# Stick-breaking scores: the second products on 64 rows, in both row halves of the TensorE array

## The chip, the cores and the metric

The kernel runs on one core of a Trainium2 chip. The metric is the device time of one execution in microseconds, lower is better. The profiler records one execution, with the start and duration of each instruction on each engine: TensorE (PE for matmuls, PEld for its weight loads), VectorE (DVE), ScalarE (ACT), GpSimd (POOL) and SyncE (SP, which issues DMAs).

## The reference

One decoder layer on a sequence of 512 tokens with 1024 channels. Two attention branches, eight heads of 64 channels each, work on the same modulated input; the change touches the second one, stick-breaking attention:

```python
z = jnp.einsum('bhqd,bhkd->bhqk', qi, k).astype(jnp.float32) * ATTN_SCALE
strict = kpos[None, :] < qpos[:, None]
log_beta = jax.nn.log_sigmoid(z)
log_one_minus = jnp.where(strict, jax.nn.log_sigmoid(-z), 0.0)
rest = lax.cumsum(log_one_minus, axis=3, reverse=True) - log_one_minus
a = jnp.where(strict, jnp.exp(log_beta + rest), 0.0)
return jnp.einsum('bhqk,bhkd->bhqd', a.astype(v.dtype), v)
```

The other branch (FoX) is softmax attention whose logits get a decay `c_t - c_s` per head. Both branches are projected, gated, merged and projected again; then come a LayerNorm, a gated MLP with a causal convolution of width 3, and a second LayerNorm. All in 32-bit floats.

## The kernel before

Every matmul operand is split in two numbers of the matmul format (fp32r): a high part, written by ScalarE (`hi_of`), and a low part, the difference to the original, written by VectorE (`lo_of`). A product is then the sum of high times high, low times high and high times low; low times low is left out. A projection (`mm3`, line 140) is three matmuls for each of eight pieces of 128 rows, each with 128 x 128 weights and 512 moving columns.

For attention scores a head has only 64 channels, so the 128 rows of the array hold two parts at once. For a stick-breaking head (`br` is 1):

- `s1`, 128 rows, from q: rows 0 to 63 the high part, rows 64 to 127 the low part (`q_half`; `s2` is the same tile).
- `m1`, 128 rows, from k: the high part twice (`k_half`).
- `m2`, 68 rows: the low part of k in rows 0 to 63, and zeros in rows 64 to 67.

The first product, `s1` by `m1` over 128 rows, gives (high q + low q) times high k. The second one, over 68 rows, adds high q times low k. The four rows beyond 64 hold the decay in the FoX branch, which shares this code; in the stick-breaking branch they are filled with zeros (`m2z` for heads 0 and 1, `m2t` for the others, which FoX heads use later).

Queries come in four blocks `i` of 128, of which causality needs 128, 256, 384 and 512 keys; the products are never narrower than 256 columns, so their widths are 256, 256, 384 and 512. They lie in three PSUM banks: bank 2 holds blocks 1 and 0, bank 0 holds block 2, bank 1 holds block 3 (`OFS`, `ROWS`). `scores` makes one bank: for each of its blocks the first product, then the second (lines 522 and 523). `sigmoids` then takes two sigmoids of a bank on ScalarE, and `scan` makes the running product and the weights on VectorE.

Heads run in order: stick-breaking 0 to 7, then FoX 0 to 7. Heads 0 and 1 are scored in a hand-written sequence before the main loop, where a helper (line 70, `Pinned`) records each engine's instructions and keeps them in program order; so their instructions appear under line 70. In the main loop each turn scores the head two ahead (`stage_a`), transposes the weights of the next head (`stage_b`, `turn`, line 585) and multiplies the present head's weights by v (`stage_c`, line 613). Between these, `fill(n)` issues n matmuls from a stream of other work: the projections of later heads, gates, branch projections. The projections' results are split as soon as they are whole (`q_evac`, `k_evac`); six matmuls later (`LEAD`) the pair's first head is scored.

Of the kernel before, what the change touches and what calls it, by code (L numbers as in the profile page):

```python
# [9 lines left out]
F32R = mybir.dt.float32r  # L10
BF16 = mybir.dt.bfloat16
AF = mybir.ActivationFunctionType
ALU = mybir.AluOpType
# [3 lines left out]
P = 128  # L17
# [31 lines left out]
def layer_kernel(ctx: ExitStack, tc: tile.TileContext, out, xT, x, crow, wa0, wa1, w1, wct, wv, bf,  # L49
# [25 lines left out]
    V, S, PE, G = Pinned(nc.vector), Pinned(nc.scalar), Pinned(nc.tensor), Pinned(nc.gpsimd)  # L75
# [10 lines left out]
    def nm(s):  # L86
        cnt[0] += 1
        return f"{s}_{cnt[0]}"

    def bank():  # L90
        return pp.tile([P, 512], F32, name=nm("ps"), tag="ps")
# [4 lines left out]
    def fl(ap):  # L96
        return ap.bitcast(F32)

    def hi_of(o, i, scale=1.0):
        S.activation(o, i, AF.Copy, scale=scale)  # L100

    def lo_of(o, i, hi):
        return V.tensor_tensor(o, i, fl(hi), ALU.subtract)  # L103
# [28 lines left out]
    def z(dt, s, shape=(P, 512)):  # L132
        return zp.tile(list(shape), dt, name=nm(s), tag="z", bufs=NZ)
# [23 lines left out]
    def weights(i, ahead=AHEAD):  # L157
        load()
        while state["proc"] < min(len(items), i + 1 + ahead):
            process()  # L160
            load()
        return items[i][4]
# [194 lines left out]
    OFS = ((2, 256), (2, 0), (0, 0), (1, 0))  # L357
    WID = (384, 512, 384)
    ORD = (1, 0, 2, 3)
    m2z = [z(F32R, "m2z", (68, 512)) for _ in range(2)]  # L360
    for t in m2z:
        G.memset(fl(t[64:68, :]), 0.0)
    ptc, s2t, m2t, chi, atp = [], [], [], [], []

    def open_att():
        att = st2.enter_context(tc.tile_pool(name="att", bufs=1, reuse_waits="tile"))
        atp.append(att)
        ptc.extend([att.tile([P, 512], F32R, name=f"ptc{i}{e}", tag=f"ptc{i}{e}") for e in range(2)] for i in range(2))
        s2t.extend(att.tile([68, 512], F32R, name=f"s2_{i}", tag=f"s2_{i}") for i in range(4))
        m2t.extend(att.tile([68, 512], F32R, name=f"m2_{i}", tag=f"m2_{i}") for i in range(4))  # L370
        chi.append(att.tile([NH, 2, 512], F32R, name="chi", tag="chi"))

    def fill_att():
        for t in ptc[0]:
            G.memset(fl(t[:, 0:128]), 0.0)
        for t in m2t[2:] + m2t[:2]:
            G.memset(fl(t[64:68, :]), 0.0)
        for t in ptc[1]:
            G.memset(fl(t[:, 0:128]), 0.0)
        for t in s2t:  # L380
            G.memset(fl(t[64:68, :]), 1.0)
            G.memset(fl(t[64:66, :]), -1.0)
# [31 lines left out]
    hd = {}  # L414
# [3 lines left out]
    def slot_free(n):  # L418
        assert n < 4 or n - 4 in scored
        return n % 4  # L420

    def idx(br, h):
        return h if br == 1 else NH + h

    def q_half(br, p, ps, hh):
        h = 2 * p + hh
        r = slice(64 * hh, 64 * hh + 64)
        s1 = z(F32R, "s1")
        hi_of(s1[0:64, :], ps[r, :], 0.125)
        d = hd.setdefault((br, h), {})  # L430
        d["s1"] = s1
        if br == 0:
            s2 = s2t[slot_free(idx(br, h))]
            G.dma_start(s2[0:64, :], s1[0:64, :])
            d["s2"] = s2
        else:
            d["s2"] = s1

        def low():
            V.scalar_tensor_tensor(s1[64:128, :], ps[r, :], 0.125, fl(s1[0:64, :]), ALU.mult, ALU.subtract)  # L440
        return low

    def k_half(br, p, ps, hh):
        h = 2 * p + hh
        r = slice(64 * hh, 64 * hh + 64)
        m1 = z(F32R, "m1")
        hi_of(m1[0:64, :], ps[r, :])
        hi_of(m1[64:128, :], ps[r, :])
        n = slot_free(idx(br, h))
        m2 = m2z[h] if br == 1 and h < 2 else m2t[n]  # L450
        lo_of(m2[0:64, :], ps[r, :], m1[0:64, :])
        d = hd.setdefault((br, h), {})
        d["m1"], d["m2"] = m1, m2

# [57 lines left out]

    ROWS = ((2,), (3,), (1, 0))

    def scores(br, h, b):
        d = hd[(br, h)]
        bk = d.setdefault("bk", {})[b] = bank()
        for i in ROWS[b]:
            o = OFS[i][1]
            w = max(256, (i + 1) * P)  # L520
            tb = slice(i * P, (i + 1) * P)
            PE.matmul(bk[:, o : o + w], d["s1"][:, tb], d["m1"][:, 0:w], start=i > 0, stop=False)  # L522
            PE.matmul(bk[:, o : o + w], d["s2"][0:68, tb], d["m2"][0:68, 0:w], start=False, stop=i != 1)  # L523

    def sigmoids(h, b):
        d = hd[(1, h)]
        bk = d["bk"].pop(b)
        om, pt = z(F32, "om"), z(F32, "pt")
        w = WID[b]
        S.activation(om[:, 0:w], bk[:, 0:w], AF.Sigmoid, scale=-1.0)  # L530
        d["last"] = S.activation(pt[:, 0:w], bk[:, 0:w], AF.Sigmoid)
        d.setdefault("om", {})[b] = om
        d.setdefault("pt", {})[b] = pt

    def scan(h, b):
        d = hd[(1, h)]
        om, pt, w = d["om"].pop(b), d["pt"][b], WID[b]
        if b == 2:
            G.memset(om[:, 256:257], 0.0)
        d0 = om[:, 1:w][:, ::-1]  # L540
        d1 = idz[:, 513 - w : 512] if b < 2 else idd[:, 1:w]
        V.tensor_tensor_scan(d0, d0, d1[:, ::-1], 0.0, ALU.mult, ALU.add)
        V.tensor_tensor(pt[:, 0 : w - 1], pt[:, 0 : w - 1], om[:, 1:w], ALU.mult)
        G.memset(pt[:, w - 1 : w], 0.0)

    def mark_scored(br, h):
        scored.add(idx(br, h))
        if br == 0 and h + 4 < NH:
            decay_rows(h + 4)
        if br == 1 and h >= 4 and gated:  # L550
            decay_rows(h - 4)

    def stage_a(br, h):
        for b in (2, 0, 1):
            scores(br, h, b)
        if br == 0:
            d = hd[(br, h)]
            bk = d.pop("bk")
            pt = d["pt"] = [z(F32, "pt"), z(F32, "pt"), z(F32, "pt")]
            sm = atp[0].tile([P, 12], F32, name=nm("sm"), tag="sm", bufs=3)  # L560
            for i in ORD:
                b, o = OFS[i]
                w = (i + 1) * P
                c = slice(o, o + w)
                V.tensor_tensor_reduce(pt[b][:, c], bk[b][:, c], negt[:, 512 - w : 512], -1.0, -NEG, ALU.add, ALU.min, sm[:, i : i + 1])
                S.activation(pt[b][:, c], pt[b][:, c], AF.Exp, bias=sm[:, i : i + 1], scale=-1.0, accum_out=sm[:, 4 + i : 5 + i])
            V.reciprocal(sm[:, 8:12], sm[:, 4:8])
            for i in ORD:
                b, o = OFS[i]
                c = slice(o, o + (i + 1) * P)  # L570
                V.tensor_scalar_mul(pt[b][:, c], pt[b][:, c], sm[:, 8 + i : 9 + i])
        else:
            for b in (2, 0, 1):
                sigmoids(h, b)
                scan(h, b)
        mark_scored(br, h)
# [271 lines left out]
    for hh in range(2):  # L848
        q_half(1, 0, grp[0], hh)()
        k_half(1, 0, grp[1], hh)  # L850
    first_mm(KT - 1, (2,))
    scores(1, 0, 2)
    first_mm(KT - 1, (7,))
    st0.close()
    open_att()
    sigmoids(0, 2)
    v_copy(0)
    scan(0, 2)
    scores(1, 0, 0)
    sigmoids(0, 0)  # L860
    scan(0, 0)
# [39 lines left out]
    for n, (b, h) in enumerate(heads):  # L901
        f1, f2, f3 = FILL[n // 8]
        if n + 2 < 16:
            if n % 2 == 0:
                fill_to(marks[(n // 2 + 1, "k")])
                fill(LEAD)
                f1 -= LEAD
            if n == 6:
                forget(hd[heads[n + 1]]["last"])
            stage_a(*heads[n + 2])  # L910
        fill(f1)
        if n + 1 < 16:
            stage_b(*heads[n + 1])
        if n == 3:
            for j in range(NB):
                v_evac(1, j, 1, vf[j])
        fill(f2)
        stage_c(b, h)
        if n == 7:
            lim[0] = marks["y0"]  # L920
        if n == 15:
            lim[0] = len(stream)
        fill(f3)
# [120 lines left out]
    for n in range(2 * FT):  # L1044
        if n < NSPLIT:
            h, l = items[wui[n]][4]
            ps = bks[n]
            up_mm(ps, h, l, slice(256, 512))
        else:
            ps = bank()  # L1050
            h, l = weights(wui[n])
# [3 lines left out]
        t = z(F32, "cv")  # L1055
# [4 lines left out]
        if n % 2 == 1:  # L1060
# [4 lines left out]
            a, b = z(F32R, "hh"), z(F32R, "hl")  # L1065
# [9 lines left out]
    for i in range(2):  # L1075
        t = fin.tile([P, D], F32, name=f"ln2_{i}", tag=f"ln2_{i}")
# [12 lines left out]
    for j in range(FT - LATE):  # L1089
        w = weights(wdi[j])  # L1090
# [4 lines left out]
    for i in range(NB):  # L1095
        tb = slice(i * P, (i + 1) * P)
        r = x1[i]
# [5 lines left out]
        for n, (e, c0, c1) in enumerate(pieces):  # L1103
            sole = (i, e) == own
            ps = bank()[:, 0 : c1 - c0] if sole else acc[i][e]
            for q in range(LATE):
                w = [ws[q][a][e][:, c0:c1] for a in range(2)]
# [8 lines left out]
        for e, c0, c1 in pieces:  # L1116
            c = slice(e * 512 + c0, e * 512 + c1)
            v = r[e][:, c0:c1]
            V.scalar_tensor_tensor(v, v, mu, lnr[0][:, c], ALU.subtract, ALU.mult)
        for e, c0, c1 in pieces:  # L1120
            c = slice(e * 512 + c0, e * 512 + c1)
# [71 lines left out]
```

## Time and profile before

| | |
|---|---|
| median of 3 runs | 753.81 us (753.63 to 754.15) |
| profiled execution, its time | 753.64 us |
| profiled execution, its span | 751.5 us |
| TensorE matmul busy | 741.8 us (99%), 3502 matmuls |
| weight loads busy | 621.0 us (83%) |
| VectorE busy | 545.4 us (73%) |
| ScalarE busy | 351.9 us (47%) |
| GpSimd busy | 126.6 us (17%) |

The span runs from the first to the last instruction of the program. Busy time is the time in which at least one instruction of the engine is on record; matmuls are pipelined, so the records of successive ones overlap, and the time that one costs is the distance to the start of the next. In a row of the timeline stand the start, the duration, the engine, the line, the operation, and what is written from what, by the program's names without their numbers (`m` stands for `m1` and `m2`, `s` for `s1` and `s2`).

### The profile page before, as it was taken

To read this page: it belongs to the slowest core of one execution; us is meant where nothing else is said; L and a number is where in the kernel's file an instruction comes from. 1 tells how busy PE (TensorE), PEld (TensorE's weight loads), DVE (VectorE), ACT (ScalarE), POOL (GpSimd) and SP (SyncE) were. 2 spreads that over 40 slices of the span, in tenths; PEclk is the share of its full clock that TensorE was granted. 3 is DMA by queue.
4 is the path that set the end of the run, shared out by engine and by line. 5 is a ranking of instruction groups with operands and counts; after the bars stand their busy time and mean duration, and the time that the engine had idled before them with its cause. 6 is when DMAs were issued, how large, how long until landed. Compare 5 with 4: busy or idle time off the path is not lost.

```text
span 751.5 us, 9515 instructions
## 1 busy us (share of the span) xinstructions
PE 741.8 (99%) x3502; PEld 621.0 (83%) x3502; DVE 545.4 (73%) x896; ACT 351.9 (47%) x587; POOL 126.6 (17%) x153
## 2 busy tenths in 40 slices
PE   9999999999999999999999999999999999999995
PEld 7888888888888888888898888888888888888885
DVE  7888989867688875596987787666755686334666
ACT  5578767468655754343246344444444442212300
POOL 2103000030110000000000690000000137454400
PEclk9999999999999999999999999999999999999998
DMA  9941332424333434565234524333333234224102
GB/s 352 405 142 70 99 139 87 157 84 168 106 114 120 154 113 168 169 232 165 86 113 140 168 94 131 139 114 133 120 117 107 85 110 149 104 86 140 56 33 79
DMA packets 31088, 100.46 MB, mean 134 GB/s; under 512 B 4113, under 2 KB 4641, under 8 KB 31042
## 3 DMA queue, kind: packets, MB, share of 16 engines
q1 hardware_dynamic: 29536, 97.69, 37.3%
q0 software_dynamic: 1504, 2.17, 1.2%
q8 instruction: 27, 0.44, 0.2%
q14 instruction: 19, 0.16, 0.1%
q10 hardware_dynamic: 2, 0.00, 0.0%
HBM read 96.63 MB, written 2.11 MB: 131 GB/s over the span
## 4 chain that ended last, share of the span: by engine, by line
PE 97%; DVE 2%; DMA 0%; ACT 0%; issue 0%; DVEq 0%
PE ps L140 56%; PE ps L330 5%; PE ps L1086 5%; PE ps L1084 5%; PE ps L1085 5%; PE ps L613 3%; PE ps L70 2%; PE ps L585 2%; PE ps L795 2%; PE ps L796 2%; PE ps L794 2%; PE ps L523 1%; PE ps L522 1%; PE ps L496 1%; PE ps L497 1%; PE ps L498 1%
## 5 line engine op out<-in xcount | busy, mean ns | idle before, releaser
L103 DVE TENSOR_TENSOR wl<-raw,wh 128x1024 fp32r<-128x1024 f32 (+1 forms) x99 | 133.2, 1346 | 55.4 <-ACT wh L100 55.2
L140 PE MATMUL ps<-u2h,wh 128*128 128x512 f32 (+1 forms) x376 | 141.2, 376 | 0.0
L140 PE MATMUL ps<-u2l,wh 128*128 128x512 f32 (+1 forms) x376 | 141.0, 376 | 0.0
L140 PE MATMUL ps<-u2h,wl 128*128 128x512 f32 (+1 forms) x376 | 133.6, 376 | 0.0
L100 ACT ACTIVATE wh<-raw 128x1024 fp32r<-128x1024 f32 (+1 forms) x99 | 103.5, 1048 | 62.7 <-PE ps L1086 46.1
L140 PE MATMUL ps<-uh,wh 128*128 128x512 f32 x213 | 84.1, 395 | 0.0
L140 PE MATMUL ps<-ul,wh 128*128 128x512 f32 x213 | 83.3, 391 | 0.0
L140 PEld LDWEIGHTS ps<-u2h,wh 128*128 128x128 f32 x376 | 70.8, 188 | 12.9
L140 PEld LDWEIGHTS ps<-u2l,wh 128*128 128x128 f32 x376 | 70.8, 188 | 12.6
L140 PEld LDWEIGHTS ps<-u2h,wl 128*128 128x128 f32 x376 | 70.4, 188 | 12.9
L140 PE MATMUL ps<-uh,wl 128*128 128x512 f32 x213 | 78.9, 390 | 0.0
L683 POOL TENSOR_TENSOR raw<-raw,gt 128x1024 f32<-128x1024 f32 x22 | 56.4, 2571 | 92.6 <-DMA raw<-in_wdn 85.0
L1057 DVE SCALAR_TENSOR_TENSOR cv<-ps,cw,cv 128x511 f32<-128x511 f32 x44 | 32.9, 748 | 53.4 <-ACT cv L1056 53.4
L1056 ACT ACTIVATE cv<-ps,cw 128x512 f32<-128x512 f32 x44 | 34.1, 776 | 45.7 <-PE ps L140 45.7
L1084 PE MATMUL ps<-wh,hh 128*128 128x512 f32 x128 | 49.8, 389 | 0.0
L1085 PE MATMUL ps<-wl,hh 128*128 128x512 f32 x128 | 49.8, 389 | 0.0
L1086 PE MATMUL ps<-wh,hl 128*128 128x512 f32 x128 | 49.8, 389 | 0.0
L140 PEld LDWEIGHTS ps<-uh,wl 128*128 128x128 f32 x213 | 40.0, 188 | 8.7
L140 PEld LDWEIGHTS ps<-uh,wh 128*128 128x128 f32 x213 | 40.0, 188 | 8.0
L140 PEld LDWEIGHTS ps<-ul,wh 128*128 128x128 f32 x213 | 40.1, 188 | 7.9
L100 ACT ACTIVATE hh<-cv 128x512 fp32r<-128x512 f32 x22 | 13.9, 633 | 57.5 <-DVE cv L1064 57.5
L216 DVE SCALAR_TENSOR_TENSOR ada<-ada,cbc 128x1024 f32<-128x1024 f32 x24 | 29.3, 1219 | 9.1 <-DMA ada<-in_wa 8.7
(245 smaller groups left out, 1428.7 us busy)
## 6 DMA issues: line engine op xcount, KB each, us to landing
raw<-in_wup SPq DMA_DIRECT2D x44, 512.0 KB, 3.4
raw<-in_wct SPq DMA_DIRECT2D x29, 512.0 KB, 3.8
ada<-in_wa SPq DMA_DIRECT2D x24, 512.0 KB, 4.3
raw<-in_wdn SPq DMA_DIRECT2D x22, 512.0 KB, 3.3
wa<-in_wa SPq DMA_DIRECT2D x16, 512.0 KB, 7.4
raw<-in_wp SPq DMA_DIRECT2D x8, 512.0 KB, 3.3
raw<-in_wo SPq DMA_DIRECT2D x8, 512.0 KB, 4.0
raw<-in_wa SPq DMA_DIRECT2D x8, 512.0 KB, 3.3
```

The source lines that it names most:

```text
L100: S.activation(o, i, AF.Copy, scale=scale)
L103: return V.tensor_tensor(o, i, fl(hi), ALU.subtract)
L140: PE.matmul(ps, w, u, start=first and n == 0, stop=last and n == 2)
L216: V.scalar_tensor_tensor(wt, wt, 1.0, cbc, ALU.mult, ALU.mult, accum_out=raw)
L330: PE.matmul(grp[g], w, u, start=j == 0 and n == 0, stop=j == KT - 1 and n == (1 if g == 7 else 2))
L613: PE.matmul(ps[:, to : to + w], v_part(br, h, j), src[e][:, so : so + w], start=a == 0 and j == 0, stop=a == 1 and j == 3)
L683: G.tensor_tensor(r, r, gt[1], ALU.mult)
L1056: S.activation(t, ps, AF.Identity, bias=cw[:, n, 3:4], scale=cw[:, n, 2:3])
L1057: V.scalar_tensor_tensor(t[:, 1:], ps[:, 0:511], cw[:, n, 1:2], t[:, 1:], ALU.mult, ALU.add)
L1084: PE.matmul(ps, hh[j][:, tb], w[0], start=first, stop=False)
L1085: PE.matmul(ps, hh[j][:, tb], w[1], start=False, stop=False)
L1086: PE.matmul(ps, hl[j][:, tb], w[0], start=False, stop=last)
```

## The change

In all stick-breaking heads the second product has 64 rows in place of 68, and the zero fills of rows 64 to 67 go. In heads 2 to 7 (`split`) the parts are also laid out so that the second products of the four blocks stand in alternating halves of the array: `s1` has, for its first 256 columns (blocks 0 and 1), the low part in rows 0 to 63 and the high part in rows 64 to 127, and for blocks 2 and 3 as before; `m2t` has 128 rows, with the low part of k a second time, for 256 columns, in rows 64 to 127. So the second products of blocks 2 and 3 use rows 0 to 63, those of blocks 1 and 0 rows 64 to 127. `scores2` issues all products of a head in an order of its own: block 1 first, 0 first, 2 first, 2 second (upper half), 1 second (lower half), 3 first, 3 second (upper), 0 second (lower). The sigmoids of heads 2 to 7 go by banks 0, 2, 1 in place of 2, 0, 1.

```diff
-    m2z = [z(F32R, "m2z", (68, 512)) for _ in range(2)]
-    for t in m2z:
-        G.memset(fl(t[64:68, :]), 0.0)
+    m2z = [z(F32R, "m2z", (64, 512)) for _ in range(2)]
...
-        m2t.extend(att.tile([68, 512], F32R, name=f"m2_{i}", tag=f"m2_{i}") for i in range(4))
+        m2t.extend(att.tile([P, 512], F32R, name=f"m2_{i}", tag=f"m2_{i}") for i in range(4))
...
-        for t in m2t[2:] + m2t[:2]:
-            G.memset(fl(t[64:68, :]), 0.0)
...
+    def split(br, h):
+        return br == 1 and h > 1
...
-        hi_of(s1[0:64, :], ps[r, :], 0.125)
         d = hd.setdefault((br, h), {})
         d["s1"] = s1
+        cut = 256 if split(br, h) else 0
+        parts = [(o, slice(a, b)) for o, a, b in ((64, 0, cut), (0, cut, 512)) if a < b]
+        for o, c in parts:
+            hi_of(s1[o : o + 64, c], ps[r, c], 0.125)
...
-            V.scalar_tensor_tensor(s1[64:128, :], ps[r, :], 0.125, fl(s1[0:64, :]), ALU.mult, ALU.subtract)
+            for o, c in parts:
+                V.scalar_tensor_tensor(s1[64 - o : 128 - o, c], ps[r, c], 0.125, fl(s1[o : o + 64, c]), ALU.mult, ALU.subtract)
...
         lo_of(m2[0:64, :], ps[r, :], m1[0:64, :])
+        if split(br, h):
+            lo_of(m2[64:128, 0:256], ps[r, 0:256], m1[64:128, 0:256])
...
+        n = 64 if br == 1 else 68
         for i in ROWS[b]:
...
+            PE.matmul(o, d["s1"][:, tb], d["m1"][:, 0:w], start=i > 0, stop=False)
+            PE.matmul(o, d["s2"][0:n, tb], d["m2"][0:n, 0:w], start=False, stop=i != 1)
+
+    def scores2(h):
+        d = hd[(1, h)]
+        bk = d["bk"] = {b: bank() for b in (2, 0, 1)}
+        for i, r in ((1, -1), (0, -1), (2, -1), (2, 0), (1, 64), (3, -1), (3, 0), (0, 64)):
+            o, tb, w = block(bk, i)
+            if r < 0:
+                PE.matmul(o, d["s1"][:, tb], d["m1"][:, 0:w], start=i > 0, stop=False)
+            else:
+                PE.matmul(o, d["s1"][r : r + 64, tb], d["m2"][r : r + 64, 0:w], start=False, stop=i != 1)
...
     def stage_a(br, h):
-        for b in (2, 0, 1):
-            scores(br, h, b)
+        if split(br, h):
+            scores2(h)
+        else:
+            for b in (2, 0, 1):
+                scores(br, h, b)
...
-            for b in (2, 0, 1):
+            for b in (0, 2, 1) if h > 1 else (2, 0, 1):
                 sigmoids(h, b)
                 scan(h, b)
```

More of the change, by code (lines that the diff above doesn't have):

```diff
@@ L513, in layer_kernel, with block @@
     ROWS = ((2,), (3,), (1, 0))
+    def block(bk, i):
+        b, o = OFS[i]
+        w = max(256, (i + 1) * P)
+        return bk[b][:, o : o + w], slice(i * P, (i + 1) * P), w
     def scores(br, h, b):
         d = hd[(br, h)]
-        bk = d.setdefault("bk", {})[b] = bank()
+        bk = d.setdefault("bk", {})
+        bk[b] = bank()
+        n = 64 if br == 1 else 68
         for i in ROWS[b]:
[L519 to L523, printed above, removed]
+            o, tb, w = block(bk, i)
[5 more added lines that the diff above has]
+        for i, r in ((1, -1), (0, -1), (2, -1), (2, 0), (1, 64), (3, -1), (3, 0), (0, 64)):
+            o, tb, w = block(bk, i)
+            if r < 0:
+                PE.matmul(o, d["s1"][:, tb], d["m1"][:, 0:w], start=i > 0, stop=False)
+            else:
+                PE.matmul(o, d["s1"][r : r + 64, tb], d["m2"][r : r + 64, 0:w], start=False, stop=i != 1)
     def sigmoids(h, b):
```

## The prediction

> **What bounds the kernel now.** I read the page first (engines, slices, chain), then the stages where stick-breaking scores are made, then TensorE's instructions in order of time.
>
> ```profile
> span 751.5 us, 9515 instructions
> PE 741.8 (99%) x3502; PEld 621.0 (83%) x3502; DVE 545.4 (73%) x896; ACT 351.9 (47%) x587; POOL 126.6 (17%) x153
> PE   9999999999999999999999999999999999999995
> PEclk9999999999999999999999999999999999999998
> PE 97%; DVE 2%; DMA 0%; ACT 0%; issue 0%; DVEq 0%
> 0.00:94.00 94.00, 92.28 (x420) 75.82 (x421) 80.43 (x151) 63.21 (x115) 17.45 (x64) 1.00 0.57 214
> 94.00:180.00 86.00, 86.00 (x428) 72.83 (x427) 69.61 (x118) 54.59 (x105) 10.09 (x32) 1.00 0.37 125
> ```
>
> The fifth line is the chain that ended last: 97% of it is TensorE. The last two lines are stages; after each stage's length stand the busy times of PE, PEld, DVE, ACT and POOL. From 94 to 180 us TensorE is never idle, at the full clock. So the end is set by how closely matmuls follow each other. A busy time can't show that, because the records overlap, so I read starts. This is the score block of head 5 in the timeline (start us, duration us, engine, line, operation, out<-in, rows and columns of the weights, shape of the moving operand, count):
>
> ```profile
> 109.58 0.39 PE L140 MATMUL ps<-ul,wh 128*128 128x512 f32 x1
> 109.81 0.28 PE L522 MATMUL ps<-m,s 128*128 128x256 f32 x1
> 109.92 0.29 PE L523 MATMUL ps<-m,s 68*128 68x256 f32 x1
> 110.04 0.29 PE L522 MATMUL ps<-m,s 128*128 128x256 f32 x1
> 110.17 0.28 PE L523 MATMUL ps<-m,s 68*128 68x256 f32 x1
> 110.28 0.34 PE L522 MATMUL ps<-m,s 128*128 128x384 f32 x1
> 110.46 0.34 PE L523 MATMUL ps<-m,s 68*128 68x384 f32 x1
> 110.64 0.40 PE L522 MATMUL ps<-m,s 128*128 128x512 f32 x1
> 110.87 0.40 PE L523 MATMUL ps<-m,s 68*128 68x512 f32 x1
> 111.11 0.40 PE L140 MATMUL ps<-uh,wh 128*128 128x512 f32 x1
> ```
>
> From start to start, 256 columns take (110.28 - 109.81) / 4 = 0.12 us, 384 take 0.18 and 512 take 0.23 to 0.24. The block takes 111.11 - 109.81 = 1.30 us. A 68-row product takes as long as a 128-row one: the unused rows save nothing. The duration of a record (0.39 for 512 columns) is 0.16 us longer than its pitch; that tail lies under the next matmul.
>
> **What the change removes.** In heads 2 to 7 the second products (L523) have 64 rows, and two of the four stand in the lower half of the array: block 1 (256 columns) behind block 2 (384), and block 0 (256) behind block 3 (512). If the halves work at once, the two 256-column products cost nothing: 2 x 0.12 = 0.24 us a head. For less: the weight loads of the second of each pair may come late.
>
> ```profile
> 109.58 0.19 PEld L522 LDWEIGHTS ps<-m,s 128*128 128x128 f32 x1
> 109.81 0.19 PEld L523 LDWEIGHTS ps<-m,s 68*128 68x128 f32 x1
> 109.92 0.19 PEld L522 LDWEIGHTS ps<-m,s 128*128 128x128 f32 x1
> ```
>
> Each load starts when the matmul ahead of it starts (109.81, 109.92), and they follow at 0.11 us. If this holds for halves too, the second of a pair starts 0.11 us after the first: the first pair then takes 0.11 + 0.11 = 0.22 in place of 0.18 + 0.12, saving 0.08; the second takes the longer of 0.22 and 0.24, saving 0.12. That is 0.20 a head. Six heads: 1.2 us, at most 1.44, and nothing if the halves don't work at once. I take 1.2, the sum by the rows of loads. The Trainium skill, page "TensorE: Matmul & The Clock Gate", Part 3, says that a load for other row groups overlaps running matmuls and that packed matmuls start some 4 ns apart; by that the saving would be about 1.4. No run here shows it.
>
> **What the change adds on TensorE.** The array passes from 128-row work to 64-row work and back. In heads 2 to 7 there are two stretches of 64 rows to a block, so 4 passages, 24 in all. Less visible: heads 0 and 1 also get 64-row second products (n is 64 wherever br is 1), and there each stands alone between 128-row products: 8 products, 16 passages, without any pairing to pay for them. So 40. No matmul of 64 rows is in this trace, so a passage has no row. The nearest rows are those where the stream breaks and a weight load can't be made ahead:
>
> ```profile
> 51.00 0.33 PE L70 MATMUL ps<-m2z,s 68*128 68x384 f32 x1
> 51.47 0.50 PE L70 MATMUL ps<-m,s 128*128 128x512 f32 x1
> 51.81 0.40 PE L70 MATMUL ps<-m2z,s 68*128 68x512 f32 x1
> 51.47 0.19 PEld L70 LDWEIGHTS ps<-m,s 128*128 128x128 f32 x1 [0.46 <-ACT pt L70]
> 59.13 1.25 PE L70 MATMUL ps<-idz,pt 128*128 128x128 f32 x10
> 60.14 0.48 PE L70 MATMUL ps<-uh,wh 128*128 128x512 f32 x1
> 60.45 0.40 PE L70 MATMUL ps<-ul,wh 128*128 128x512 f32 x1
> ```
>
> The load at 51.47 waited for ScalarE. Its matmul then took 51.81 - 51.47 = 0.34 to the next start, against 0.23: a load that isn't hidden costs 0.11. Behind the ten transposes (59.13) it is 60.45 - 60.14 = 0.31, so 0.08. Bounds of a passage: nothing, if the next load and matmul run on as now (a gain is excluded, since a passage takes no column away); and 0.16 + 0.11 = 0.27, if the next load waits until the last record has ended (0.39 - 0.23 = 0.16) and then is itself exposed. I take 0.11, the nearest row and near the middle. Two passages, around head 0's 384-column product at 51.00, lie ahead of the 0.46 us for which loads wait anyway; 38 are on the path: 38 x 0.11 = 4.2 us.
>
> **What it adds and moves elsewhere.** The rows are from the same timeline (in brackets the idle time before and what ended it), the last one from the groups by line. Per split head: one more ScalarE instruction (the high part of q in two halves of 256), and two more on VectorE (the low part of q in two, and low k once more for 256 columns).
>
> ```profile
> 62.34 1.18 ACT L70 ACTIVATE s<-ps 64x512 fp32r<-64x512 f32 x2
> 66.03 1.41 DVE L70 SCALAR_TENSOR_TENSOR s<-ps,s 64x512 fp32r<-64x512 f32 x2
> 67.46 0.68 DVE L70 TENSOR_TENSOR m<-ps,m 64x512 fp32r<-64x512 f32 x1
> 68.18 1.20 ACT L70 ACTIVATE m<-ps 64x512 fp32r<-64x512 f32 x2 [3.44 <-DVE m L70]
> 69.90 1.32 ACT L70 ACTIVATE vv<-vf 128x256 fp32r<-128x256 f32 x4
> 70.34 1.43 DVE L70 TENSOR_TENSOR vv<-vf,vv 128x256 fp32r<-128x256 f32 x4 [0.23 <-ACT vv L70]
> 70.37 0.29 PE L523 MATMUL ps<-m,s 68*128 68x256 f32 x1
> 102.52 1.13 DVE L543 TENSOR_TENSOR pt<-pt,om 128x383 f32<-128x383 f32 x2
> 114.58 1.25 PE L585 MATMUL ps<-idz,pt 128*128 128x128 f32 x10
> L523 PEld LDWEIGHTS ps<-m,s 68*128 68x128 f32 x56 | 10.5, 190 | 0.9 <-DVE m L103 0.5
> ```
>
> At 256 columns ScalarE takes 1.32 / 4 = 0.33 and VectorE 1.43 / 4 = 0.36. Head 2 is the tightest: its low k ends at 67.46 + 0.68 = 68.14 and is first used at 70.37, so 2.2 us stand between. The new VectorE work ahead of it is 4 x 0.36 - 1.41 = 0.03 for both heads' q and 0.36 for k, so 0.4; even if a 256-column instruction cost as much as one of 512 columns (0.70), it would be 4 x 0.70 - 1.41 + 0.68 = 2.1. ScalarE's two further instructions (4 x 0.33 - 1.18 = 0.14) fall before its wait of 3.44. Over six heads VectorE gets some 2.2 us in stretches where it is 81% (69.61 of 86) busy, and loads of L523 waited for it only 0.5 us in all 56. I cost this at nothing; without its cover it would be at most those 2.2 us.
>
> The order of products and of sigmoids changes: block 2's bank is now whole first, at 0.12 + 0.12 + 0.18 + 0.18 = 0.6 us after the block's start in place of 0.48 for the first bank, and the others at the end. Attention weights of head 4 (scored at 97 us) are ready at 102.52 + 1.13 = 103.65 and transposed at 114.58: 10.9 us of cover for some tenths. The six zero fills of four rows that go were on POOL, busy 17%; nothing waits for them on the path, so nothing is gained. No DMA is added, and neither SP's nor POOL's queue is passed by one.
>
> **Sum.** -1.2 + 4.2 = +3.0 us. The profiled execution took 753.64 us, 2.1 more than its span of 751.5; it becomes 756.6. The median of the runs shown, 753.81, lies 0.17 above it: 756.8.
>
> **Rivals.**
> *A, the passages cost nothing (not slower).* For it: 68-row products follow 128-row ones without any break (109.92, 110.17), and TensorE's loads already run under other matmuls. Against it: those 68-row records keep the pitch of the whole array, so they don't show a passage. It decides from 1.2 / 38 = 0.03 us a passage down; at nothing the time is 753.8 - 1.2 = 752.6, at best 752.4.
> *B, each passage waits for the array to run empty.* A matmul then starts where the one ahead ends: 38 x 0.16 = 6.1, less 1.2, so +4.9 and 758.7; with the load exposed too, 38 x 0.27 = 10.3, so +9.1 and 762.9. For it: nothing in the rows; against it: no other change of shape in the trace (transposes to matmuls) costs as much. The Trainium skill, page "TensorEngine Tiling (Array Packing)", section "Tiling Modes", says that a change of the mode, not of the tile, drains the engine; by that rule B would be the outcome. No run here shows it.
> *C, the change doesn't do what it says:* the halves run one after the other. Then +4.2 and 758.0, or 753.8 if passages are free.
> *D, VectorE's added work becomes the bound:* score loads wait for low k, up to the 2.2 us that VectorE gets over six heads; with free passages 753.8 - 1.2 + 2.2 = 754.8. Against it: the slack of 2.2 us at the tightest head, where only 0.4 is added.
>
> **How the numbers follow.** Two tenths of a per cent, 1.5 us, is what a measurement of this kernel can tell from no change. Chances: forecast 0.37, own range 754.5 to 757.9 (passages of 0.05 to 0.14); A 0.35; B 0.15; C 0.09; D 0.04. Slower from (1.5 + 1.2) / 38 = 0.07 us a passage: 0.33 of the forecast, all of B, 0.06 of C and 0.01 of D, 0.55. Within: 0.04 of the forecast, 0.21 of A, and the rest of C and D, 0.31. Faster by more than 1.5 needs A with nearly all of 1.44 and a little besides: 0.14. The range goes from A's best, 752.3, to beyond B's smaller price, 759.8; B's larger price and a few tails, under 0.2, are left out.
>
> **What will show it.** In a block of heads 2 to 7: the two 64-row records of a pair start within 0.05 us of each other if the halves work at once and the loads come early, 0.11 apart if each waits for its load, 0.18 and 0.23 if the halves take turns. The block now lasts 1.30 us; 1.10 without passages' cost, 1.54 by forecast (4 x 0.11), 1.7 to 2.2 by B. In heads 0 and 1, the start after each 64-row product: 0.12, 0.18 or 0.23 if free. VectorE's waits by score loads should stay near 0.5 us. A passage price under 0.07 us, or a saving larger than 0.24 us a head, makes the forecast wrong.

## The result and the profile after

The changed kernel takes 758.88 us (median of 6 runs, 758.61 to 759.09) against 754.01 for the kernel before beside it: a ratio of 1.0063, 95% interval 1.0051 to 1.0076. It is slower by 4.9 us. The page, its first lines and its chain:

```profile
span 757.2 us, 9533 instructions
PE 747.8 (99%) x3502; PEld 620.4 (82%) x3502; DVE 550.3 (73%) x908; ACT 354.4 (47%) x593; POOL 124.5 (16%) x147
PE 98%; DVE 1%; issue 0%; DVEq 0%; ACT 0%
```

The number of matmuls is the same, the span is 5.7 us longer and TensorE's busy time 6.0. TensorE is still the chain. So its own stream became longer; busy time even counts the loss as work. The score block of head 5, in the timeline (matmuls first, then weight loads; `x2`, `x3` are records that overlap, merged):

```profile
113.72 0.39 PE L140 MATMUL ps<-ul,wh 128*128 128x512 f32 x1
113.95 0.57 PE L541 MATMUL ps<-m,s 128*128 128x256 f32 x3
114.45 0.44 PE L543 MATMUL ps<-m,s 64*128 64x384 f32 x2
114.82 0.49 PE L541 MATMUL ps<-m,s 128*128 128x512 f32 x1
115.24 0.50 PE L543 MATMUL ps<-m,s 64*128 64x512 f32 x2
115.67 0.50 PE L140 MATMUL ps<-uh,wh 128*128 128x512 f32 x1
116.01 0.40 PE L140 MATMUL ps<-ul,wh 128*128 128x512 f32 x1
113.72 0.53 PEld L541 LDWEIGHTS ps<-m,s 128*128 128x128 f32 x3
114.44 0.19 PEld L543 LDWEIGHTS ps<-m,s 64*128 64x128 f32 x2 [0.19 <-issue]
114.81 0.19 PEld L541 LDWEIGHTS ps<-m,s 128*128 128x128 f32 x1 [0.18 <-issue]
115.24 0.19 PEld L543 LDWEIGHTS ps<-m,s 64*128 64x128 f32 x2 [0.24 <-issue]
115.67 0.19 PEld L140 LDWEIGHTS ps<-uh,wh 128*128 128x128 f32 x1 [0.24 <-issue]
115.78 0.19 PEld L140 LDWEIGHTS ps<-ul,wh 128*128 128x128 f32 x1
```

Both things happen. The pairs run at once: two loads of 0.19 us stand within 0.19 us, and two matmuls, of 384 and 256 columns, within the 0.44 of the longer. And at each passage (114.44, 114.81, 115.24, 115.67) the load no longer starts with the matmul ahead, to run under it: it starts together with the matmul that needs it, behind a gap that no wait explains ("issue"). The block, 1.30 us before, takes 115.67 - 113.95 = 1.72, and the projection behind it starts with an exposed load (one that no matmul hides): 116.01 - 115.67 = 0.34 in place of 0.24, 0.10 more. That is 0.52 a head.

In heads 0 and 1, where nothing runs at once, the passages stand alone:

```profile
50.12 0.28 PE L70 MATMUL ps<-m,s 128*128 128x256 f32 x1
50.32 0.38 PE L70 MATMUL ps<-m2z,s 64*128 64x256 f32 x1
50.63 0.38 PE L70 MATMUL ps<-m,s 128*128 128x256 f32 x1
50.95 0.38 PE L70 MATMUL ps<-m2z,s 64*128 64x256 f32 x1
51.26 0.50 PE L70 MATMUL ps<-uh,fpad 128*128 128x512 f32 x1
51.59 0.40 PE L70 MATMUL ps<-ul,fpad 128*128 128x512 f32 x1
```

256 columns, 0.12 us before, now take 0.31 to 0.32 from start to start, in both directions (the first, whose own load is still hidden, 0.20). The first products of heads 0 and 2 in the kernel before, then head 2's in the changed one:

```profile
49.87 0.28 PE L70 MATMUL ps<-m,s 128*128 128x256 f32 x1
70.26 0.28 PE L522 MATMUL ps<-m,s 128*128 128x256 f32 x1
72.92 0.57 PE L541 MATMUL ps<-m,s 128*128 128x256 f32 x3
```

From head 0's first product to head 2's first, 70.26 - 49.87 = 20.39 us before, it is now 72.92 - 50.12 = 22.80: 2.4 us lost. With 6 x 0.52 = 3.1 that makes 5.5, and the 0.25 by which head 0 starts later in this execution makes the 5.7 of the span. The median lost 4.9: the kernel before was profiled in one of its faster executions, and the time of an execution beyond its span is shorter in the changed kernel (758.99 - 757.2 = 1.8 us, against 753.64 - 751.5 = 2.1).

### The profile page after: what moved, and what is told of

Read it like the earlier page. It is cut to its first block, busy times and chain, and to the rows that moved or that the text cites. A ratio compares the mean times of both kernels' runs of the same rounds, so it can differ in the third digit from the quotient of the medians.

```text
span 757.2 us, 9533 instructions
## 1 busy us (share of the span) xinstructions
PE 747.8 (99%) x3502; PEld 620.4 (82%) x3502; DVE 550.3 (73%) x908; ACT 354.4 (47%) x593; POOL 124.5 (16%) x147
## 4 chain that ended last, share of the span: by engine, by line
PE 98%; DVE 1%; issue 0%; DVEq 0%; ACT 0%
PE ps L140 56%; PE ps L330 5%; PE ps L1107 5%; PE ps L1108 5%; PE ps L1109 5%; PE ps L70 4%; PE ps L636 3%; PE ps L608 2%; PE ps L819 2%; PE ps L818 2%; PE ps L817 2%; PE ps L501 1%; PE ps L502 1%; PE ps L503 1%; PE ps L533 1%; PE ps L532 1%
```

## The experiments

Three theories. P: each passage between 128-row and 64-row work costs some 0.2 us and each pair at once saves its shorter product. E: the loss comes from the added evacuations, the orders and VectorE's lateness. H: pairs, or the lower half, are slow themselves. First, the number of passages was changed.

**Heads 0 and 1 with 68 rows again** (24 passages)

```diff
-    m2z = [z(F32R, "m2z", (64, 512)) for _ in range(2)]
+    m2z = [z(F32R, "m2z", (68, 512)) for _ in range(2)]
+    for t in m2z:
+        G.memset(fl(t[64:68, :]), 0.0)
...
-        n = 64 if br == 1 else 68
+        n = 68
```

> The changed kernel, but heads 0 and 1 with 68-row second products again (zero rows and their fills included). Theory P (passages): each passage between 128-row and 64-row work costs 0.20 us, read off the changed trace as 0.09 us until the next weight load starts and 0.11 us for the load itself, and each pair at once saves 0.12 us. 24 passages are left of 40: 24 x 0.20 - 12 x 0.12 = +3.3 us against the kernel before, so 2.4 us faster than the changed one in its trace's terms. Theory E (the loss comes from the added evacuations, the order of sigmoids and lateness on VectorE): heads 0 and 1 have none of it, so the loss stays, +4.9. Theory H (the pairs, or the lower half, are slow themselves): stays +4.9.

Measured: 757.04 us against 754.28, ratio 1.0031 (1.0019 to 1.0042), +2.8. Of the loss of 4.9, 2.1 was in heads 0 and 1, where the change takes away four rows and their zero fills and does nothing else. P expected 2.4; E and H expected no change to the changed kernel.

**One stretch of 64 rows a head** (28 passages)

```diff
-        for i, r in ((1, -1), (0, -1), (2, -1), (2, 0), (1, 64), (3, -1), (3, 0), (0, 64)):
+        for i, r in ((1, -1), (0, -1), (2, -1), (3, -1), (2, 0), (1, 64), (3, 0), (0, 64)):
```

> The changed kernel, but scores2 issues the four first products, then the four second ones: one stretch of 64 rows a head in place of two. 28 passages. Theory P: 12 x 0.20 = 2.4 us faster than the changed kernel; against the kernel before +3.6 by the trace's sum (2.7 of heads 0 and 1, 12 x 0.20 - 1.44 = 1.0 of the others). Inside the stretch block 3's second product follows block 2's without a gap. Theory E: no change to the changed kernel, +4.9. Theory H: the same products and pairs, +4.9.

Measured: 756.66, ratio 1.0029 (1.0020 to 1.0039), +2.4. That is 2.5 less than the changed kernel's 4.9, where P expected 2.4 less and E and H no change; P's +3.6 against the kernel before is 1.2 too high. Its timeline, the block of head 5:

```profile
113.65 0.81 PE L541 MATMUL ps<-m,s 128*128 128x256 f32 x4
114.39 0.67 PE L543 MATMUL ps<-m,s 64*128 64x384 f32 x4
114.99 0.50 PE L140 MATMUL ps<-uh,wh 128*128 128x512 f32 x1
115.33 0.40 PE L140 MATMUL ps<-ul,wh 128*128 128x512 f32 x1
```

The block takes 114.99 - 113.65 = 1.34 in place of 1.72: two passages less are worth 0.38. The four 64-row products take 0.60 together, load and gap included, so there is nothing to pay inside a stretch.

**Both** (12 passages)

> Both edits together: 12 passages. Theory P: 12 x 0.20 - 12 x 0.12 = +1.0 us against the kernel before, within what is called no change. Theory E: +4.9. Theory H: about +4.9 less what heads 0 and 1 bring.

Measured: 754.40, ratio 1.0001 (0.9992 to 1.0009). It can't be told from the kernel before. P expected +1.0, and with 0.19 a passage its sum is 12 x 0.19 - 1.44 = 0.8; the interval ends at +0.7, just below (the table in the next section shows where the rest lies). This kernel keeps all of the layout and the pairs, so E and H, which expected a loss of several us, fall.

**The kernel before with 64 rows, nothing else** (64 passages)

```diff
-            PE.matmul(bk[:, o : o + w], d["s2"][0:68, tb], d["m2"][0:68, 0:w], start=False, stop=i != 1)
+            PE.matmul(bk[:, o : o + w], d["s2"][0 : 64 + 4 * (br == 0), tb], d["m2"][0 : 64 + 4 * (br == 0), 0:w], start=False, stop=i != 1)
```

> The kernel before, with one edit: 64 rows in place of 68 in the second products of all stick-breaking heads; no other layout, order or evacuation. Each of 32 products stands alone: 64 passages, no pairs. Theory P: heads 0 and 1 as in the changed kernel, 2.7, and 48 x 0.20 = 9.5, together +12.1 us, so 766. Theory E: no loss, 754.0. Theory H: no product at once with another and none in the lower half, so no loss, 754.0.

Measured: 765.84, ratio 1.0148 (1.0134 to 1.0162), +11.6. This edit takes work away (four rows) and adds no instruction. Its timeline, the block of head 2:

```profile
72.76 0.28 PE L522 MATMUL ps<-m,s 128*128 128x256 f32 x1
72.96 0.38 PE L523 MATMUL ps<-m,s 64*128 64x256 f32 x1
73.28 0.38 PE L522 MATMUL ps<-m,s 128*128 128x256 f32 x1
73.59 0.38 PE L523 MATMUL ps<-m,s 64*128 64x256 f32 x1
73.90 0.44 PE L522 MATMUL ps<-m,s 128*128 128x384 f32 x1
74.27 0.44 PE L523 MATMUL ps<-m,s 64*128 64x384 f32 x1
74.64 0.49 PE L522 MATMUL ps<-m,s 128*128 128x512 f32 x1
75.06 0.50 PE L523 MATMUL ps<-m,s 64*128 64x512 f32 x1
75.49 0.50 PE L140 MATMUL ps<-uh,wh 128*128 128x512 f32 x1
75.83 0.40 PE L140 MATMUL ps<-ul,wh 128*128 128x512 f32 x1
72.96 0.18 PEld L523 LDWEIGHTS ps<-m,s 64*128 64x128 f32 x1 [0.24 <-issue]
73.90 0.19 PEld L522 LDWEIGHTS ps<-m,s 128*128 128x128 f32 x1
```

From 72.76 to 75.83 are 3.07 us, against 1.30 + 0.23 before: 1.54 for 8 passages, 0.19 each, whatever the width. A passage has two parts, which the first and the last step show one at a time. The load of the first product (72.76) was still hidden, and yet 72.96 - 72.76 = 0.20 us pass until the next load and its matmul start, in place of 0.12: 0.08 us until the array takes a load of the other kind. Behind the projection at 75.49 there is no passage, and yet it takes 75.83 - 75.49 = 0.34 in place of 0.23: 0.11 for its own load, which nothing covers.

**Pairs in the same half** (40 passages, nothing at once)

```diff
-        cut = 256 if split(br, h) else 0
+        cut = 0
...
-        for i, r in ((1, -1), (0, -1), (2, -1), (2, 0), (1, 64), (3, -1), (3, 0), (0, 64)):
+        for i, r in ((1, -1), (0, -1), (2, -1), (2, 0), (1, 0), (3, -1), (3, 0), (0, 0)):
```

> The changed kernel with its order and its 64 rows, but all second products of heads 2 to 7 in rows 0 to 63 (q laid out as before, low k's second copy still made), so that the two of a stretch come one after the other in the same half. 40 passages as in the changed kernel. Theory P: the 12 shorter products cost their 0.12 us again, +1.4 us against the changed kernel, some 760.3; the second load of a stretch is hidden under the first product. If the pairs bring less (by the load 0.11 behind, as the prediction took it), +1.2. Theory H (pairs or the lower half slow): not slower than the changed kernel.

Here q's parts are written whole again, too. Measured: 760.65, ratio 1.0086 (1.0072 to 1.0100), +6.7. Its timeline, head 5:

```profile
115.45 0.57 PE L541 MATMUL ps<-m,s 128*128 128x256 f32 x3
115.95 0.55 PE L543 MATMUL ps<-m,s 64*128 64x384 f32 x2
116.43 0.50 PE L541 MATMUL ps<-m,s 128*128 128x512 f32 x1
116.86 0.62 PE L543 MATMUL ps<-m,s 64*128 64x512 f32 x2
117.40 0.50 PE L140 MATMUL ps<-uh,wh 128*128 128x512 f32 x1
```

The block takes 1.95, 0.23 to 0.24 more than in the changed kernel: the pairs save just the two shorter products. H falls again.

**All but the 64 rows, and its two parts.** Added evacuations, product order and sigmoid order, with 68-row products (the rows of heads 0 and 1 and the zero fills are left out here):

```diff
...
-        parts = [(o, slice(a, b)) for o, a, b in ((64, 0, cut), (0, cut, 512)) if a < b]
+        parts = [(o, slice(a, b)) for o, a, b in ((0, 0, cut), (0, cut, 512)) if a < b]
...
-            lo_of(m2[64:128, 0:256], ps[r, 0:256], m1[64:128, 0:256])
+            lo_of(m2[0:64, 0:256], ps[r, 0:256], m1[64:128, 0:256])
...
-        for i, r in ((1, -1), (0, -1), (2, -1), (2, 0), (1, 64), (3, -1), (3, 0), (0, 64)):
+        for i, r in ((1, -1), (0, -1), (2, -1), (2, 0), (1, 0), (3, -1), (3, 0), (0, 0)):
...
-                PE.matmul(o, d["s1"][r : r + 64, tb], d["m2"][r : r + 64, 0:w], start=False, stop=i != 1)
+                PE.matmul(o, d["s1"][r : r + 68, tb], d["m2"][r : r + 68, 0:w], start=False, stop=i != 1)
```

> All of the change but the 64 rows: the product order of scores2, the order 0, 2, 1 of the sigmoids, q's parts written in two halves of 256 columns and low k's 256 columns written a second time (over the same rows), with 68-row second products in the upper rows and the zero fills as before. No passages, no pairs. Theory P: as the kernel before within 0.5 us, 754.0 to 754.5. Theory E (added evacuations and order): up to the 1.3 us that the median of only passages and pairs may leave, 755 or more.

Measured: 754.72, ratio 1.0009 (1.0000 to 1.0018), +0.75. That lies between P's 754.0 to 754.5 and E's 755. The blocks take 1.30 as before, but there is one stall. TensorE's timeline, then VectorE's:

```profile
129.12 0.93 PE L612 MATMUL ps<-idz,pt 128*128 128x128 f32 x7
131.11 0.52 PE L612 MATMUL ps<-idz,pt 128*128 128x128 f32 x3 [1.05 <-DVE yf L647]
126.02 2.49 DVE L103 TENSOR_TENSOR wvl<-raw,wvh 128x512 fp32r<-128x512 f32 x4
129.00 1.23 DVE L216 SCALAR_TENSOR_TENSOR ada<-ada,cbc 128x1024 f32<-128x1024 f32 x1 [0.49 <-DMA ada<-in_wa]
130.27 0.69 DVE L647 TENSOR_TENSOR yf<-ps,ytmp 64x512 f32<-64x512 f32 x1
```

The last three transposes wait for a bank that `yf` empties, and `yf` stands on VectorE behind a modulation product (`ada`), which itself waits for its DMA. In the kernel before (the first two rows) and in the changed kernel (the last two), `yf` comes ahead of it:

```profile
125.30 0.69 DVE L620 TENSOR_TENSOR yf<-ps,ytmp 64x512 f32<-64x512 f32 x1
129.65 1.20 DVE L216 SCALAR_TENSOR_TENSOR ada<-ada,cbc 128x1024 f32<-128x1024 f32 x1
130.59 0.69 DVE L643 TENSOR_TENSOR yf<-ps,ytmp 64x512 f32<-64x512 f32 x1
131.67 1.23 DVE L216 SCALAR_TENSOR_TENSOR ada<-ada,cbc 128x1024 f32<-128x1024 f32 x1 [0.38 <-DMA ada<-in_wa]
```

The two parts of that experiment, each as an edit of it. First the orders alone:

```diff
-        parts = [(o, slice(a, b)) for o, a, b in ((0, 0, cut), (0, cut, 512)) if a < b]
+        parts = [(o, slice(a, b)) for o, a, b in ((0, 0, 512),) if a < b]
...
-        if split(br, h):
-            lo_of(m2[0:64, 0:256], ps[r, 0:256], m1[64:128, 0:256])
```

Then the evacuations alone:

```diff
-        if split(br, h):
-            scores2(h)
-        else:
-            for b in (2, 0, 1):
-                scores(br, h, b)
+        for b in (2, 0, 1):
+            scores(br, h, b)
...
-            for b in (0, 2, 1) if h > 1 else (2, 0, 1):
+            for b in (2, 0, 1):
```

> rest_alone without its added evacuations: only the product order of scores2 and the order 0, 2, 1 of the sigmoids, with 68-row products. In rest_alone TensorE's transposes wait 1.2 us at 130 us for a bank that VectorE empties behind a modulation product (ada), which is 1 us late for VectorE's added work. Theory V (VectorE's added work makes that wait): none here, 754.0 within 0.4 us, and the step from head 6's block to head 7's is 12.6 us as before. Theory O (the new order makes it): the wait of some 1.2 us is here, 13.8 us from block to block, 754.7 or more.

> rest_alone without its orders: only q's parts in two halves of 256 columns and low k's second copy; products and sigmoids in the order of the kernel before. Theory V: the wait of some 1.2 us at 130 us stays, 13.8 us from head 6's block to head 7's, 754.7 or more. Theory O: no wait, 12.6 us, 754.0 within 0.4 us.

Measured: 754.49 for the orders, ratio 1.0002 (0.9993 to 1.0010), and 754.06 for the evacuations, 0.9999 (0.9990 to 1.0008). The starts of two score blocks in the traces:

| | head 6 | head 7 | step |
|---|---|---|---|
| kernel before | 125.20 | 137.84 | 12.64 us |
| orders alone | 125.88 | 138.49 | 12.61 us |
| evacuations alone | 125.47 | 138.36 | 12.89 us |
| both | 125.77 | 139.62 | 13.85 us |
| changed kernel | 129.83 | 142.99 | 13.16 us |

So neither theory holds as put: the evacuations alone bring 0.25 us of the stall, and its full size of 1.2 needs both. With the evacuations alone the modulation product also stands ahead of `yf` (127.75 and 129.01); in all kernels but these two `yf` comes first. None of the three medians is clear of no change (the one with both just touches it); the stall itself stands in the traces. In the changed kernel the step is 13.16, that is 12.64 and the block's 0.52, without a stall.

## Why the prediction was right or wrong

The forecast was 3.0 us slower, 756.8; the kernel became 4.9 us slower, 758.88, by what the forecast added up: passages, less the products that run at once. One term of that sum had the wrong size.

**What bounds the kernel: right.** TensorE stayed the chain, and the loss is in its start-to-start times alone.

**The saving: right in kind, a little small.** I took 1.2 us because I let the second load of a pair start 0.11 us behind the first. The loads start together (at 114.44, two records within 0.19 us), and against the pairs in the same half the block is 1.95 - 1.72 = 0.23 us shorter: nearly the full 0.24 a head, 1.4 in all. Here the rule that I set beside the sum (the Trainium skill, page "TensorE: Matmul & The Clock Gate", Part 3) was the better guide: by it the saving was an estimated 1.4, and the trace agrees.

**The passages: right in kind and number, the price mis-sized.** This is the term that failed. The forecast took 0.11 us, an exposed load, for 38 passages: 4.2. Measured are 0.19: the load, 0.11, and 0.08 ahead of it, which the forecast left out. In heads 2 to 7, 24 x 0.19 = 4.6; in heads 0 and 1, 2.4, where 16 x 0.19 would be 3.0 and the rest falls where TensorE waited or a load was exposed already (I had counted two passages as covered). Together 7.0 - 1.44 = 5.5 in the trace, against 3.0 forecast. That heads 0 and 1 pay without any gain, which the prediction read off the code, was 2.4 of the 5.5.

**Rival B named the mechanism, with another size.** At a passage the next load does wait, and it is exposed too. But the wait is 0.08, not the 0.16 by which a matmul's record outlasts its pitch: with 64 rows only, the load at 73.90 starts before the record of the matmul ahead ends (73.59 + 0.38 = 73.97), so the end of a record is no measure of when the array takes the next load. With 0.08 + 0.11 for both parts, the sum 38 x 0.19 - 1.44 = 5.8 would have come near the trace's 5.5. The Trainium skill, page "TensorEngine Tiling (Array Packing)", section "Tiling Modes", says that a change of mode drains TensorE; the trace agrees in that the next load starts 0.08 us after the last column (0.20 in place of 0.12), where other loads start with the matmul ahead.

The measured 758.88 lies outside the range that I gave the forecast itself (754.5 to 757.9), and 0.2 from B's smaller sum, 758.7. That nearness is luck: B's sum has a wait of 0.16 and no exposed load, and the time beyond the span, which no sum of mine held, took 0.35 us off the loss. I should have given more than 0.15 to the case in which both parts are paid.

**A, C and D fell:** passages cost; the halves do work at once; and score loads waited 0.5 us in all for low parts on VectorE, as before.

**The cover of the added work: right for this kernel, thinner than I said.** The added records on VectorE last 3.5 us in all, not 2.2: 2.5 for low k's six copies and 0.9 for q's halves. (The page's busy time rose by 550.3 - 545.4 = 4.9, but that is no measure of added work: it rose by 6.7, to 552.1, in the kernel before with 64 rows only, which has no added instruction.) I took 0.36 us for 256 columns from four `vv` records that overlap, 0.34 from start to start; each of them lasts 0.42 too, and the new ones don't overlap:

```profile
66.78 1.75 DVE L70 SCALAR_TENSOR_TENSOR s<-ps,s 64x256 fp32r<-64x256 f32 x4
68.56 1.13 DVE L70 TENSOR_TENSOR m<-ps,m 64x512 fp32r<-64x512 f32 x2
```

1.75 / 4 = 0.44 in place of 0.36, and 1.13 - 0.68 = 0.45 for low k's copy. Head 2's low k was still ready at 68.56 + 1.13 = 69.69, 3.2 us before the head's block at 72.92. But I looked at the scores alone; the place where the added work reached TensorE is a PSUM bank at 130 us that VectorE has to empty, and there another order of two VectorE instructions cost 0.25 us in one experiment and 1.2 in another.

One thing stays open in part: the medians of all six kernels with passages lie 0.1 to 0.8 us below the sums of their blocks. The traces agree with these sums within 0.3 us: here each is compared with the kernel before, from the first score product to the end of the span. The sum is what the blocks of heads 0 to 7 take longer, with the exposed load behind them.

| kernel | passages | median, longer by | trace, longer by | sum of its blocks |
|---|---|---|---|---|
| both (68 rows, one stretch) | 12 | 0.1 us | 1.0 us | 0.8 us |
| heads 0 and 1 with 68 rows | 24 | 2.8 us | 3.4 us | 3.1 us |
| one stretch a head | 28 | 2.4 us | 3.0 us | 3.2 us |
| changed kernel | 40 | 4.9 us | 5.5 us | 5.5 us |
| pairs in the same half | 40 | 6.7 us | 6.8 us | 6.9 us |
| 64 rows, nothing else | 64 | 11.6 us | 11.5 us | 11.6 us |

In the kernel with both, 0.28 us of the trace is a wait of head 2's scores for a bank that ScalarE empties. What the medians miss lies in part beyond the span: in every kernel that writes low k's second copy the time beyond the span is 1.8 us, in the others (the kernel before, 64 rows only, the orders alone) 2.1 to 2.2. Why it is shorter isn't shown. Another part is that the kernel before was profiled in one of its shorter executions: its span there is 751.5 us, and the medians of its runs beside the experiments are 751.8 to 752.1. Its first score product starts at 49.87 us in that profile, and at up to 50.96 in the other traces; what moves it was not tried.

## What to carry to other kernels

Count the passages between 128-row and 64-row matmuls, in each direction, before counting columns saved: at 0.19 us each a stretch of 64 rows has to save more than 0.39 us, by estimate some 830 columns at 0.12 us for 256, and here it saved 0.12 (two stretches a head) or 0.24 (one). A lone product of 64 rows is better padded with zeros past 64: 68 rows ran at the pitch of 128. And when a change splits evacuations, look for the PSUM banks that the same engine empties later, not only for the consumers of what it writes.

## What the runs showed of the hardware that I had not expected

Taking four rows from each of 32 products made the kernel slower by 11.6 us (64 passages). Two loads into the two halves take the time of one: 0.19 us for both records. Within a stretch of 64 rows, a product in the same half costs its usual time (0.23 to 0.24 us a block for two of 256 columns). And at a passage the exposed load shows in the records as a matmul that starts together with its load and lasts 0.11 us longer (0.50 in place of 0.39), mostly with "issue" as all that is named for the gap before.
